# The first two sums of a seven-product weight chunk, formed ahead of the splits and into a tile of their own

## The chip, the cores and the metric

One core of one Trainium2 chip runs the whole program in one launch. The metric is the device time of an execution in microseconds (us), less being better. Five engines work side by side, each on its own queue and in the order of that queue: PE (TensorE, the matmuls; PEld is its loading of stationary operands), DVE (VectorE), ACT (ScalarE), POOL (GpSimd) and SP (SyncE, which here only issues transfers). An instruction that has to wait holds up all that stands behind it on the same engine. SBUF is the on-chip memory with 128 partitions, PSUM the banks into which matmuls accumulate.

## The reference

The kernel computes one layer on 256 tokens of width 2048, in float32: a token mixer with retention (8 heads) beside a gated linear recurrence, a merge of the two, an attention over 256 memory tokens, and a gated convolutional feed-forward part of width 5632. Nearly all of its arithmetic is products of a 256-row activation with a large weight matrix:

```python
q, k, v, g_ret, xr, yr, g_a, g_b = jnp.split(hn @ w_in[l], offsets, axis=-1)
...
merged = (jax.nn.sigmoid(g_a) * (ret_out @ w_proj_ret[l])
          + jax.nn.sigmoid(g_b) * (rnn_out @ w_proj_rnn[l]))
h = h + merged @ w_mix_out[l]
...
h = h + memory_cross_attention(hn, mem_n, xa_w_q[l], xa_w_k[l], xa_w_v[l], xa_w_o[l])
...
h = h + conv_gated_ffn(hn, ffn_w_up[l], ffn_conv_w[l], ffn_conv_b[l], ffn_w_down[l])
return rmsnorm(h, final_norm_w)
```

## The kernel before

**Products.** A weight chunk is loaded as float32 into a tile `raw`. Every value is split into two parts that a matmul can take: ACT copies it into the shorter type (`hi`, line 451), and DVE subtracts that from the value (`lo`, line 452). This is `weight_parts`. Activations are split likewise (`s`, `ts`). A product of two split operands costs three matmuls of 512 columns: high by high, low by high, high by low. The last of the three reads the weight's `lo`.

**Pairs and seven-product chunks.** Most weights are taken two column blocks of 512 at a time (`pair`, `steps_pair`). A chunk of such a pair holds two row tiles of 128 by two column blocks, four blocks in all. An ordinary chunk needs eight products, 24 matmuls. In chunks that the table `MARKS` names, the 2-by-2 product is formed with seven products, 21 matmuls, from sums of the blocks; the activation's sums (`ts`, made through a small tile `tq`) are formed by `sums_of`, the weight's by DVE. Where DVE and ACT form the weight's sums from the loaded chunk alone, `seven_parts` does it: 49 chunks. (Two other kinds get some sums by a transfer that adds; they are not touched.) In a seven-product chunk `raw` holds b11, b12, b22, b21. The seven pairs of parts are used by PE in the order p1, p3, p2, q1, q3, q2, q4. p1, p3 and p2 are splits of b11, b22 and b21; q1 and q3 split b11+b12 and b12+b22; q2 and q4 split the two sums that are built on those.

**Buffers.** `raw` has 3 buffers, `hi` and `lo` 6 each. A chunk's load is asked for on SP two chunks ahead, and it can start when DVE has formed the last `lo` from the buffer's chunk of three before. The pool `tp` gives all small temporary tiles named `tmp` (2 KB a partition each): `tq`, the two parts of attention probabilities `ps`, the junk output of squares `junk`, the gated product `ft` and `fo`, and others.

**Order.** Matmuls keep the order of the program. DVE, ACT, POOL and SP get their order from a scheduler that goes by its own estimate of durations, by priorities and by which buffers it takes to be free, so a small edit can move instructions far from it.

**Ends of pairs.** When a pair of column blocks is done, DVE gathers the banks (`o`, lines 627 and 638, called `o` in the profile). A result that the next product needs as its left operand is turned: `by_dma` has ACT split it into half words (`pl`, line 664), SP issues a transposing transfer for each 128 rows (`pt`, line 665), and ACT joins the halves again (`f`, line 677) before they are split into `s`. At the merge, lines 1083 and 1140 stand between the gathering and `pl`; at a residual, line 1155 adds the result to the stream (`nat`), and `squares` (line 1176, `junk`) takes the row sums.

Of the kernel before, what the change touches and what calls it, by code (L numbers as in the profile page):

```python
# [9 lines left out]
F32 = mybir.dt.float32  # L10
# [4 lines left out]
ALU = mybir.AluOpType  # L15
AX = mybir.AxisListType

P = 128
# [10 lines left out]
BW = 512  # L29
KC = 4  # L30
KH = 2
# [168 lines left out]
def hybrid_layer(  # L200
# [17 lines left out]
    act, dve, pe, pool, sp = nc.scalar, nc.vector, nc.tensor, nc.gpsimd, nc.sync  # L218

    cp = ctx.enter_context(tc.tile_pool(name="cp", bufs=1))  # L220
    wp = ctx.enter_context(tc.tile_pool(name="wp", bufs=2))
    bp = ctx.enter_context(tc.tile_pool(name="bp", bufs=31))
    tp = ctx.enter_context(tc.tile_pool(name="tp", bufs=7))
    sp_ = ctx.enter_context(tc.tile_pool(name="sp", bufs=2))
    pm = ctx.enter_context(tc.tile_pool(name="pm", bufs=3, space=bass.MemoryType.PSUM))
    px = ctx.enter_context(tc.tile_pool(name="px", bufs=2, space=bass.MemoryType.PSUM))
# [3 lines left out]
    def nm(s):  # L230
        count[0] += 1
        return f"{s}_{count[0]}"

    def big(shape, dt=F32, s="b"):
        return bp.tile(shape, dt, tag="big", name=nm(s))
# [120 lines left out]
    def prefetch(n):  # L356
        while len(ahead) < n and taken[0] < len(stream):
# [72 lines left out]
            if isinstance(c, tuple) and c[2] == 1:  # L430
                ahead.append(((row, c), seven_parts(raw)))
                continue
# [13 lines left out]
    def weight_parts(src, pieces_=None):  # L446

        n = src.shape[1]
        hi, lo = (wp.tile([P, KH, BW], F32R, tag=a, bufs=PART_BUFS, name=nm(a)) for a in ("hi", "lo"))
        for cs in pieces_ or (slice(0, n),):  # L450
            act.copy(hi[:, cs], src[:, cs])  # L451
            dve.tensor_tensor(out=lo[:, cs], in0=src[:, cs], in1=hi[:, cs].bitcast(F32), op=ALU.subtract)  # L452
        return [(hi[:, i, :], lo[:, i, :]) for i in range(n)]
# [12 lines left out]
    def seven_parts(raw):  # L466

        b11, b12, b22, b21 = (raw[:, i : i + 1, :] for i in range(4))
        p1, p3 = weight_parts(raw[:, 0:3:2])
        (p2,) = weight_parts(raw[:, 3:4])  # L470
        two = b12.to_broadcast([P, 2, BW])
        for o, a, b in ((raw[:, 0:2], two, raw[:, 0:3:2]), (b22, b11, b22), (b21, b22, b21)):
            dve.tensor_tensor(out=o, in0=a, in1=b, op=ALU.add)  # L473
        q1, q3 = weight_parts(raw[:, 0:2])
        q2, q4 = weight_parts(raw[:, 2:4])
        return [p1, p3, p2, q1, q3, q2, q4]

# [62 lines left out]
    def gemm_n(*args):  # L540
        return ended(steps_n(*args))
# [98 lines left out]
    def pair(*args):  # L640
        return ended(steps_pair(*args))
# [284 lines left out]
    for g in range(2):  # L926
        dec = big([P, 4, S], s="dec")
        vs, turned = [], ([], [])
        for b, o in enumerate((O_Q, O_K)):
# [6 lines left out]
            if b and not g and paired():  # L936
                a, v = pair("w_in", 0, xs, NT, O_K, O_V + BW)
                scaled(a, rs0)
                by_dma(a, rotate_both)
            else:  # L940
                a = gemm_n("w_in", 0, xs, NT, o + g * BW) if g + b else q0
                turned_rows(a, rs0, rotate_both, 2 - b if g + b else 3, g + b > 0, LAG["by_rotate"])
            if b == 1:
                sp.dma_start(
                    out=dec,
# [11 lines left out]
        for a in pair("w_in", 0, xs, NT, c, c + BW):  # L957
            t = big([P, 2, BW], s="gate")
# [466 lines left out]
    for kind, b, *n in ff_plan():  # L1425
# [5 lines left out]
        else:  # L1431
            final = b + n[0] == NF // 4
            if final:
                wfin = []
                for i in range(2):
                    t = big([P, 2, BW], s="wf")
                    sp.dma_start(
                        out=t.rearrange("p a n -> p (a n)"),
# [42 lines left out]
```

## Time and profile before

| | |
|---|---|
| median of 3 runs | 1955.75 us (1953.15 to 1957.33) |
| the profiled execution | 1956.59 us, of which its span 1954.5 us |
| PE busy | 1944.4 us, 99%, 8735 matmuls |
| DVE busy | 1659.0 us, 85% |
| ACT busy | 1457.7 us, 75% |
| POOL busy | 68.5 us, 4% |
| read from memory | 407.27 MB, 209 GB/s over the span |
| chain that ended last | PE 88%, DVE 5%, ACT 3%, DMA 2% |

The span runs from the first to the last instruction that the profiler saw; 2.1 us of the profiled execution lie around it. Busy time is the union of an engine's instructions. A matmul's end is modelled and overlaps the start of the next one, so a short pause between two matmuls may not show as idle time. In a row of the timeline the columns are the start, the length, the engine, the line, the operation, what it writes and reads, and how many like it follow each other without a break; in brackets stands the idle time ahead of it and what ended it. A group's row gives its total, the mean of one in ns, and the idle time ahead.

### The profile page before, as it was taken

The page shows a single profiled execution, that of the slowest core. Times are in us where ns is not written, and L with a number is a line of the kernel's source. Part 1 is how long each engine was busy: PE and PEld are TensorE (multiplying, and loading weights), DVE is VectorE, ACT ScalarE, POOL GpSimd, SP SyncE. Part 2 cuts the span into 40 slices and gives each one's busy share as a digit, 9 for nine tenths or more (in the row PEclk, how much of TensorE's full clock was granted, in tenths as well). Part 3 has the DMA queues.
Part 4 walks back from the last instruction along what each step waited for, and adds up shares of the span by engine and source line. Part 5 has one row for each costly group of instructions (what it writes and reads, how often), then busy time and mean ns, then how long its engine had stood idle before and what let it go on. Part 6 is the DMA issues. An engine that isn't in the chain of part 4 may idle for free.

```text
span 1954.5 us, 24287 instructions
## 1 busy us (share of the span) xinstructions
PE 1944.4 (99%) x8735; PEld 1612.9 (83%) x8735; DVE 1659.0 (85%) x2155; ACT 1457.7 (75%) x1792; POOL 68.5 (4%) x69
## 2 busy tenths in 40 slices
PE   9999999999999999999999999999999999999998
PEld 7888888888888888888888888888887888888887
DVE  6887987787889988887888857789999889999986
ACT  6665758999756666778678777888877578884784
POOL 0000001000100000000000000000000000000000
PEclk9999999999999999999999999999999999999999
DMA  8866767666867786778868687676677877678773
GB/s 332 262 215 198 245 222 217 213 218 229 237 217 265 233 264 215 253 253 252 247 213 239 223 221 225 226 232 226 211 224 224 269 248 221 223 224 271 230 255 119
DMA packets 211352, 454.99 MB, mean 233 GB/s; under 512 B 143264, under 2 KB 147872, under 8 KB 170400
## 3 DMA queue, kind: packets, MB, share of 16 engines
q1 hardware_dynamic: 204896, 430.38, 66.5%
q0 software_dynamic: 6336, 23.07, 6.3%
q8 instruction: 68, 1.11, 0.2%
q14 instruction: 52, 0.43, 0.1%
HBM read 407.27 MB, written 2.10 MB: 209 GB/s over the span
## 4 chain that ended last, share of the span: by engine, by line
PE 88%; DVE 5%; ACT 3%; DMA 2%; issue 2%; POOL 0%; SPq 0%; POOLq 0%; DVEq 0%; ACTq 0%
PE acc L285 63%; PE sm L285 26%; DVE lo L452 2%; ACT hi L451 1%; DMA raw<-in_wall 1%; ACT f L677 1%; DVE o L627 1%; ACT pl L664 0%; DMA fl<-fr 0%; DVE o L638 0%; DMA pt<-pl 0%; DVE raw L473 0%; DVE fv L1282 0%; DVE fg L1282 0%; DVE s L702 0%
## 5 line engine op out<-in xcount | busy, mean ns | idle before, releaser
L452 DVE TENSOR_TENSOR lo<-raw,hi 128x1024 fp32r<-128x1024 f32 (+1 forms) x824 | 940.4, 1169 | 203.0 <-ACT hi L451 193.0
L285 PE MATMUL acc<-hi,s 128*128 128x512 f32 x3526 | 1081.5, 388 | 0.4 <-ACT s L727 0.2
L451 ACT CAST hi<-raw 128x1024 fp32r<-128x1024 f32 (+1 forms) x824 | 801.1, 1007 | 301.9 <-DMA raw<-in_wall 83.1
L285 PEld LDWEIGHTS acc<-hi,s 128*128 128x128 f32 x3526 | 659.5, 188 | 136.1 <-DVE s L728 0.6
L285 PE MATMUL acc<-lo,s 128*128 128x512 f32 x1727 | 669.7, 388 | 0.1
L285 PE MATMUL sm<-hi,s 128*128 128x512 f32 x1464 | 450.9, 389 | 0.0
L285 PEld LDWEIGHTS acc<-lo,s 128*128 128x128 f32 x1727 | 324.4, 188 | 68.6 <-DVE lo L452 2.1
L285 PEld LDWEIGHTS sm<-hi,s 128*128 128x128 f32 x1464 | 274.7, 188 | 57.2 <-ACT prob L1203 0.2
L285 PE MATMUL sm<-lo,s 128*128 128x512 f32 x720 | 280.3, 389 | 0.0
L677 ACT COPY f<-pt 128x1024 uint16<-128x1024 uint16 x128 | 166.8, 1353 | 10.0 <-DMA pt<-pl 10.0
L285 PEld LDWEIGHTS sm<-lo,s 128*128 128x128 f32 x720 | 135.2, 188 | 28.6 <-DVE lo L452 0.6
L285 PE MATMUL acc<-hi,ts 128*128 128x512 f32 x438 | 134.9, 389 | 0.0
L473 DVE TENSOR_TENSOR raw<-raw 128x1024 f32<-128x1024 f32 x147 | 127.1, 865 | 1.9
L285 PEld LDWEIGHTS acc<-hi,ts 128*128 128x128 f32 x438 | 82.2, 188 | 17.0
L285 PE MATMUL acc<-lo,ts 128*128 128x512 f32 x219 | 85.7, 391 | 0.7 <-DVE lo L452 0.6
L664 ACT COPY pl<-o 128x1024 uint16<-128x1024 uint16 x64 | 62.5, 1040 | 3.7 <-DVE o L638 2.8
L330 POOL DMA_DIRECT2D tw<-in_wall x24 | 21.4, 891 | 980.8 <-DMA tw<-in_wall 355.7
L285 PEld LDWEIGHTS acc<-lo,ts 128*128 128x128 f32 x219 | 41.1, 188 | 10.8 <-DVE lo L452 2.4
L664 ACT COPY pl<-rows 128x1024 uint16<-128x1024 uint16 x44 | 43.7, 1044 | 7.6 <-DVE rows L694 7.6
L1421 ACT ACTIVATE o<-o,ro 128x512 f32<-128x512 f32 x44 | 30.1, 718 | 23.9 <-DVE o L638 23.8
L638 DVE TENSOR_TENSOR o<-o,sm 128x512 f32<-128x512 f32 x64 | 42.2, 679 | 3.9 <-PE sm L285 3.9
L285 PE MATMUL sm<-hi,ts 128*128 128x512 f32 x146 | 45.0, 389 | 0.0
(197 smaller groups left out, 1321.2 us busy)
## 6 DMA issues: line engine op xcount, KB each, us to landing
raw<-in_wall SPq DMA_DIRECT2D x319, 1024.0 KB, 5.1
raw<-in_wall SPq DMA_DIRECT2D x24, 768.0 KB, 5.6
tw<-in_wall SPq DMA_DIRECT2D x24, 512.0 KB, 7.7
tw<-in_wall POOLq DMA_DIRECT2D x24, 512.0 KB, 7.3
raw<-in_wall SPq DMA_DIRECT2D x13, 512.0 KB, 6.6
fr<-in_wall SPq DMA_DIRECT2D x12, 512.0 KB, 7.4
fl<-fr POOLq DMA_DIRECT2D x12, 512.0 KB, 8.1
nat<-in_x SPq DMA_DIRECT2D x8, 512.0 KB, 9.7
```

The source lines that it names most:

```text
L285: tc.keep_in_program_order(pe.matmul(*a, **k))
L330: pool.dma_start(out=far[i], in_=source(i)[:, 0:KH, :], accum_op=ALU.add)
L451: act.copy(hi[:, cs], src[:, cs])
L452: dve.tensor_tensor(out=lo[:, cs], in0=src[:, cs], in1=hi[:, cs].bitcast(F32), op=ALU.subtract)
L473: dve.tensor_tensor(out=o, in0=a, in1=b, op=ALU.add)
L627: dve.tensor_tensor(out=o, in0=a, in1=b, op=op)
L638: dve.tensor_tensor(out=o, in0=o, in1=a, op=ALU.add)
L664: act.copy(planes[:, tt], words[:, tt])
L677: act.copy(halves_[:, :, :, cs], turned_[:, :, :, cs])
L1421: act.mul(a[:, tt, :], a[:, tt, :], rs2[:, tt : tt + 1])
```

## The change

`seven_parts` now begins with the two first sums, b11+b12 and b12+b22, in one DVE instruction of the same shape as before, and writes them into a new tile `t13` (128 by 1024 float32, 4 KB a partition, one buffer). Before, they were formed after the splits of p1, p3 and p2 and overwrote b11 and b12. The two later sums are as before, but the first of them reads b11+b12 from `t13`. q1 and q3 are split from `t13`. The pool of small temporary tiles goes from 7 to 5, which frees as much memory as the new tile takes. No instruction is added or removed.

```diff
-    tp = ctx.enter_context(tc.tile_pool(name="tp", bufs=7))
+    tp = ctx.enter_context(tc.tile_pool(name="tp", bufs=5))
...
         b11, b12, b22, b21 = (raw[:, i : i + 1, :] for i in range(4))
+        t = wp.tile([P, KH, BW], F32, tag="t13", bufs=1, name=nm("t13"))
+        dve.tensor_tensor(out=t, in0=b12.to_broadcast([P, KH, BW]), in1=raw[:, 0:3:2], op=ALU.add)
         p1, p3 = weight_parts(raw[:, 0:3:2])
         (p2,) = weight_parts(raw[:, 3:4])
-        two = b12.to_broadcast([P, 2, BW])
-        for o, a, b in ((raw[:, 0:2], two, raw[:, 0:3:2]), (b22, b11, b22), (b21, b22, b21)):
-            dve.tensor_tensor(out=o, in0=a, in1=b, op=ALU.add)
-        q1, q3 = weight_parts(raw[:, 0:2])
+        for o, x, y in ((b22, t[:, 0:1], b22), (b21, b22, b21)):
+            dve.tensor_tensor(out=o, in0=x, in1=y, op=ALU.add)
+        q1, q3 = weight_parts(t)
         q2, q4 = weight_parts(raw[:, 2:4])
```

The order of the matmuls stays. DVE, ACT, SP and, in one place, POOL get another order, and not only inside `seven_parts`. Lines behind the edit count one higher afterwards. Three places follow.

The first is the merge, ahead of the first product with `w_mix_out` (at 805 us in the trace of before). DVE before (o_6749 is the result that is turned first, raw_6852 an ordinary chunk, raw_6886 a seven-product one):

```order
L638 TENSOR_TENSOR o_6749<-o_6749,acc_6498 128x1024
L1140 TENSOR_TENSOR o_6750<-o_6750,o_5363 128x1024
L1083 SCALAR_TENSOR_TENSOR o_6749<-o_6109,o_6749 128x1024
L452 TENSOR_TENSOR lo_6855<-raw_6852,hi_6854 128x1024
L1140 TENSOR_TENSOR o_6749<-o_6749,o_5362 128x1024
L452 TENSOR_TENSOR lo_6859<-raw_6852,hi_6858 128x1024
L452 TENSOR_TENSOR lo_6889<-raw_6886,hi_6888 128x1024
```

And now on DVE (o_6762 is that result, raw_6865 and raw_6899 the two chunks):

```order
L639 TENSOR_TENSOR o_6762<-o_6762,acc_6510 128x1024
L1141 TENSOR_TENSOR o_6763<-o_6763,o_5372 128x1024
L1084 SCALAR_TENSOR_TENSOR o_6762<-o_6120,o_6762 128x1024
L452 TENSOR_TENSOR lo_6872<-raw_6865,hi_6871 128x1024
L1141 TENSOR_TENSOR o_6762<-o_6762,o_5371 128x1024
L470 TENSOR_TENSOR t_1325_6901<-raw_6899 128x1024
L452 TENSOR_TENSOR lo_6904<-raw_6899,hi_6903 128x1024
```

The ordinary chunk's second `lo` has moved ahead of the merge's last addition, and the first sum stands ahead of its chunk's first `lo`. On SP, a chunk's load that stood between the two transposes of this result now stands ahead of both.

The second place is the first residual (at 850 us). DVE before (o_7018 and nat_6931 belong to the column block that is turned first, raw_7242 and raw_7321 are seven-product chunks):

```order
L638 TENSOR_TENSOR o_7018<-o_7018,acc_6849 128x1024
L559 TENSOR_TENSOR tq_7182<-g_7179,tq_7182 128x128
L1155 TENSOR_TENSOR nat_6931<-nat_6931,o_7018 128x1024
L562 TENSOR_TENSOR ts_7181<-tq_7182,ts_7181 128x512
L452 TENSOR_TENSOR lo_7215<-raw_7208,hi_7214 128x1024
L452 TENSOR_TENSOR lo_7245<-raw_7242,hi_7244 128x1024
L473 TENSOR_TENSOR raw_7242<-raw_7242 128x1024
L473 TENSOR_TENSOR raw_7242<-raw_7242 128x512
L452 TENSOR_TENSOR lo_7249<-raw_7242,hi_7248 128x512
L473 TENSOR_TENSOR raw_7242<-raw_7242 128x512
L452 TENSOR_TENSOR lo_7256<-raw_7242,hi_7255 128x1024
```

And now on DVE (nat_6945, raw_7256 and raw_7336 are the same three):

```order
L639 TENSOR_TENSOR o_7032<-o_7032,acc_6862 128x1024
L452 TENSOR_TENSOR lo_7229<-raw_7222,hi_7228 128x1024
L1156 TENSOR_TENSOR nat_6945<-nat_6945,o_7032 128x1024
L470 TENSOR_TENSOR t_1397_7258<-raw_7256 128x1024
L452 TENSOR_TENSOR lo_7261<-raw_7256,hi_7260 128x1024
L474 TENSOR_TENSOR raw_7256<-t_1397_7258,raw_7256 128x512
L452 TENSOR_TENSOR lo_7265<-raw_7256,hi_7264 128x512
L474 TENSOR_TENSOR raw_7256<-raw_7256 128x512
L452 TENSOR_TENSOR lo_7271<-t_1397_7258,hi_7270 128x1024
L729 SCALAR_TENSOR_TENSOR s_7383<-xt_7041,pb,s_7383 128x256
L470 TENSOR_TENSOR t_1412_7338<-raw_7336 128x1024
L452 TENSOR_TENSOR lo_7275<-raw_7256,hi_7274 128x1024
```

The residual's addition now stands behind one more `lo` (and behind the split of `ts`, above these rows), and the next seven-product chunk's first sum stands ahead of this chunk's last `lo`. Of the 49 first sums, 24 stand ahead of at least one `lo` of an earlier chunk in this way.

ACT at the same place, before:

```order
L451 CAST hi_7244<-raw_7242 128x1024
L664 COPY pl_7192<-nat_6931 128x1024 x2
L664 COPY pl_7199<-nat_7025 128x1024 x2
L451 CAST hi_7248<-raw_7242 128x512
L451 CAST hi_7255<-raw_7242 128x1024
L1176 ACTIVATE junk_7470,ss_6848<-nat_6931 128x512
L1176 ACTIVATE junk_7472,ss_6848<-nat_6931 128x512
L1176 ACTIVATE junk_7508,ss_6848<-nat_7025 128x512
L451 CAST hi_7259<-raw_7242 128x1024
```

And now on ACT:

```order
L451 CAST hi_7260<-raw_7256 128x1024
L665 COPY pl_7206<-nat_6945 128x1024 x2
L451 CAST hi_7264<-raw_7256 128x512
L665 COPY pl_7213<-nat_7039 128x1024 x2
L451 CAST hi_7270<-t_1397_7258 128x1024
L1177 ACTIVATE junk_7486,ss_6861<-nat_6945 128x512
L728 ACTIVATE s_7383<-xt_7041,pb 128x256
L451 CAST hi_7274<-raw_7256 128x1024
```

Two of the squares have moved back, behind the rows shown, and one cast has moved in between the two pairs of `pl`.

The third place is an end of a pair in the feed-forward part (at 1624 us). DVE before (raw_13732 is the first chunk of the next pair, o_13713 and o_13712 the results of the pair that ends):

```order
L452 TENSOR_TENSOR lo_13735<-raw_13732,hi_13734 128x1024
L562 TENSOR_TENSOR ts_13674<-tq_13675,ts_13674 128x512
L627 TENSOR_TENSOR o_13713<-o_13712,acc_13539 128x512
L1282 SCALAR_TENSOR_TENSOR fv_13117<-f_13658,pf,fv_13117 128x254
L627 TENSOR_TENSOR o_13712<-o_13713,acc_13540 128x512
L1291 TENSOR_TENSOR fo_13726<-ft_13725,fv_13117 128x512
L627 TENSOR_TENSOR o_13713<-acc_13540,o_13712 128x512
L627 TENSOR_TENSOR o_13713<-acc_13540,o_13713 128x512
L638 TENSOR_TENSOR o_13713<-o_13713,sm_13449 128x512
L638 TENSOR_TENSOR o_13713<-o_13713,sm_13448 128x512
L702 TENSOR_TENSOR s_13729<-fo_13726,s_13729 128x2x256
L452 TENSOR_TENSOR lo_13739<-raw_13732,hi_13738 128x1024
```

And now on DVE (lo_13773 is the former lo_13735):

```order
L563 TENSOR_TENSOR ts_13712<-tq_13713,ts_13712 128x512
L628 TENSOR_TENSOR o_13751<-o_13750,acc_13576 128x512
L1283 SCALAR_TENSOR_TENSOR fv_13152<-f_13696,pf,fv_13152 128x254
L628 TENSOR_TENSOR o_13750<-o_13751,acc_13577 128x512
L1292 TENSOR_TENSOR fo_13764<-ft_13763,fv_13152 128x512
L628 TENSOR_TENSOR o_13751<-acc_13577,o_13750 128x512
L628 TENSOR_TENSOR o_13751<-acc_13577,o_13751 128x512
L703 TENSOR_TENSOR s_13767<-fo_13764,s_13767 128x2x256
L639 TENSOR_TENSOR o_13751<-o_13751,sm_13484 128x512
L639 TENSOR_TENSOR o_13751<-o_13751,sm_13485 128x512
L452 TENSOR_TENSOR lo_13773<-raw_13770,hi_13772 128x1024
```

The next pair's first `lo` has moved from ahead of the gathering to behind it.

## The prediction

> **What bounds the kernel now.** I read the page's busy times first, then the windows of start, body and end, then the chain, and then the matmuls' starts in the timeline.
>
> ```profile
> PE 1944.4 (99%) x8735; PEld 1612.9 (83%) x8735; DVE 1659.0 (85%) x2155; ACT 1457.7 (75%) x1792; POOL 68.5 (4%) x69
> ...
> 0.00:15.00 15.00, 13.71 (x53) 10.72 (x54) 8.54 (x19) 9.00 (x18) 0.97 (x7) 1.00 0.85 298
> 15.00:1940.00 1925.00, 1923.39 (x8625) 1595.11 (x8624) 1644.65 (x2117) 1446.40 (x1772) 65.30 (x58) 1.00 0.73 233
> 1940.00:1955.00 15.00, 7.32 (x62) 7.11 (x60) 5.82 (x22) 2.25 (x4) 2.21 (x4) 0.90 0.36 140
> ...
> 96.18 2.72 PE sm L285 x12
> ...
> 212.49 0.49 PE L285 MATMUL acc<-lo,s 128*128 128x512 f32 x1
> 212.82 0.62 PE L285 MATMUL acc<-hi,s 128*128 128x512 f32 x2
> ...
> 1531.88 0.61 PE L285 MATMUL acc<-hi,ts 128*128 128x512 f32 x2
> 1532.87 0.50 PE L285 MATMUL acc<-lo,ts 128*128 128x512 f32 x1 [0.38 <-DVE lo L452]
> ```
>
> The second number of a window is its length, the third PE's busy time. Of the 10.1 us in which PE is idle, 1.3 lie in the first 15 us and 7.7 in the last 15 (the output); the body has 1.6. The chain's row gives the pace: 12 matmuls in 2.72 us, 0.227 each. A matmul is drawn 0.39 long, so a pause can hide 0.16. I therefore counted starts: between 15 and 1940 us, 21 pauses bring consecutive starts 0.3 us or more apart, the first at 212.49, the last the one behind 1532.87. Their excess over 0.227 adds up to 4.1 us. That is all that better supply of PE can win: 0.21% of the time. The change neither removes matmuls nor moves them, and 0.2%, 3.9 us, is about what a measurement of this kernel can tell from no change.
>
> The Trainium skill's page "Perfetto Trace Analysis", section "Identifying the Most-Contended Engine", says that the matmul busy share is no good measure of how close PE is to its roofline, since pipelined matmuls look smaller in the trace. By that rule the 99% would leave more to win; the pace of the starts, which needs no ends, says that it doesn't here.
>
> **What the change costs inside a chunk: nothing.** The durations:
>
> ```profile
> L452 DVE TENSOR_TENSOR lo<-raw,hi 128x1024 fp32r<-128x1024 f32 x745 | 889.4, 1220 | 199.5 <-ACT hi L451 189.7 <-PE acc L285 4.2 <-PE sm L285 2.1
> L473 DVE TENSOR_TENSOR raw<-raw 128x512 f32<-128x512 f32 x98 | 67.3, 687 | 1.4
> L473 DVE TENSOR_TENSOR raw<-raw 128x1024 f32<-128x1024 f32 x49 | 59.8, 1219 | 0.5
> ...
> DVE lo L452 <- ACT hi L451: 195.4, 139, 6.7
> ACT hi L451 <- DVE raw L473: 45.0, 40, 4.5
> ```
>
> 49 first sums of 1.22 us, 98 others of 0.69: the same instructions before and after, on operands of the same size. What is gained is overlap. The first sum no longer waits for ACT's cast, so DVE can use the 1.05 us that ACT needs, where it now stands (195 us of such waits), and ACT waits less for sums (45 us). What is lost is that p1's and p3's `lo` come one sum, 1.2 us, later, with PE using them first. DVE works on a chunk for 4 wide instructions (the first sum and the `lo`s of p1 with p3, q1 with q3, q2 with q4) x 1.22 and 3 narrow ones (`lo` of p2, two sums) x 0.69, 6.9 us; its 21 matmuls take 21 x 0.227 = 4.8. So where DVE works just ahead of PE, it is the late parts, q1 to q4, that PE is likely to wait for, and those come no later. Only where PE stands does either matter.
>
> **A gain of 0.5 us at 1532.** Here two seven-product chunks follow each other, starting with a late landing:
>
> ```profile
> 1518.96 1.05 ACT L451 CAST hi<-raw 128x1024 fp32r<-128x1024 f32 x1 [5.67 <-DMA raw<-in_wall]
> 1529.86 1.06 ACT L451 CAST hi<-raw 128x1024 fp32r<-128x1024 f32 x1 [2.30 <-PE acc L285]
> ...
> 1520.04 1.23 DVE L452 TENSOR_TENSOR lo<-raw,hi 128x1024 fp32r<-128x1024 f32 x1 [3.28 <-ACT hi L451]
> 1531.60 4.77 DVE L452 TENSOR_TENSOR lo<-raw,hi 128x1024 fp32r<-128x1024 f32 x4
> ```
>
> DVE runs without a break from 1520.04 to the `lo` at 1531.60 that ends the pause at 1532.87. With the first sum at 1518.96 it is 1.08 us ahead. But the cast that goes before that `lo` gets its buffer from PE at 1529.86, so the `lo` ends no earlier than 1529.86 + 1.06 + 1.22 = 1532.14 against 1532.82: 0.68 earlier, of which the pause (0.76 less 0.23) takes 0.5.
>
> **A loss of 0.5 us at the merge.** One `lo` moved ahead of the last addition there.
>
> ```profile
> 804.67 1.22 DVE L1140 TENSOR_TENSOR o<-o,o 128x1024 f32<-128x1024 f32 x1
> ...
> 805.92 3.89 ACT L664 COPY pl<-o 128x1024 uint16<-128x1024 uint16 x4 [0.80 <-DVE o L1140]
> 816.50 1.35 ACT L677 COPY f<-pt 128x1024 uint16<-128x1024 uint16 x1 [1.48 <-DMA pt<-pl]
> ...
> 806.99 1.23 SPq L665 DMA_TRANSPOSE pt<-pl  x1
> 808.32 0.53 SPq L256 DMA_DIRECT2D raw<-in_wall  x1
> ...
> 820.16 1.01 PE L285 MATMUL acc<-hi,s 128*128 128x512 f32 x2
> ```
>
> This is the only place where the whole chain DVE, `pl`, transposes, `f`, split ends at a waiting PE (820.16, two matmuls in 1.01 where 0.62 is usual). The addition comes one `lo` pitch, 1.13 us, later. The load that SP issues between the two transposes (0.53 and its gaps, 0.6) moves ahead of both, where its buffer is free before `pl` is. So the second transpose starts 1.13 - 0.6 = 0.5 late, and PE with it. Bounds: -0.6, if the load's traffic is out of the way sooner, and 1.2.
>
> **A loss of 0.6 us behind the residual.** `nat` now stands behind a `lo` and a split of `ts`:
>
> ```profile
> 847.71 1.21 DVE L1155 TENSOR_TENSOR nat<-nat,o 128x1024 f32<-128x1024 f32 x1
> 848.85 0.68 DVE L562 TENSOR_TENSOR ts<-tq,ts 128x512 fp32r<-128x512 f32 x1
> 849.45 2.35 DVE L452 TENSOR_TENSOR lo<-raw,hi 128x1024 fp32r<-128x1024 f32 x2
> ...
> 849.31 3.88 ACT L664 COPY pl<-nat 128x1024 uint16<-128x1024 uint16 x4
> 854.57 0.62 ACT L1176 ACTIVATE junk<-nat 128x512 f32<-128x512 f32 x1
> 860.32 1.36 ACT L677 COPY f<-pt 128x1024 uint16<-128x1024 uint16 x1
> 870.36 1.99 ACT L451 CAST hi<-raw 128x1024 fp32r<-128x1024 f32 x2
> ...
> 871.42 2.36 DVE L452 TENSOR_TENSOR lo<-raw,hi 128x1024 fp32r<-128x1024 f32 x2
> ...
> 872.71 0.50 PE L285 MATMUL acc<-lo,ts 128*128 128x512 f32 x1
> ```
>
> `nat` ends 0.60 + 1.13 = 1.73 later, at 850.65, and `pl` starts 1.34 later than 849.31. From there ACT works almost without a break to the cast at 870.36, whose `lo` (end 872.65) PE takes at 872.71. Two of four squares (0.62 each) now stand behind that cast: 1.34 - 1.24 = 0.1 later. But the transposes start 1.34 later too. If the second half needs 7.6 us from issue to `f`, as at the merge (808.90 to 816.50), `f` starts at 860.6 rather than about 859.9, another 0.7 (0.2 if it is quicker). Together 0.3 to 0.9; 0.6. Bounds -0.3 (the pause of 0.1 goes) and 2.
>
> **A loss of 0.4 us at 1630.** The next pair's first `lo` moved behind the gathering:
>
> ```profile
> 1623.59 1.22 DVE L452 TENSOR_TENSOR lo<-raw,hi 128x1024 fp32r<-128x1024 f32 x1
> 1630.51 1.22 DVE L452 TENSOR_TENSOR lo<-raw,hi 128x1024 fp32r<-128x1024 f32 x1
> ...
> 1630.26 0.39 PE L285 MATMUL acc<-lo,s 128*128 128x512 f32 x1
> ```
>
> The first row is that `lo`, the second the next one. Without the first, DVE gets through the same work 1.13 sooner than 1630.51: the moved `lo` runs from 1629.38 to 1630.60 and PE, which takes it at 1630.26, waits 0.4. The second then ends at 1631.7, as before.
>
> **Elsewhere** I take 0.3: other `lo`s that moved back by 0.5 to 1.6 us reach PE with as much or more to spare, a few with 0.1 to 0.4. Cover: had PE not the parts ready some microseconds ahead, each moved sum would cost its 1.2.
>
> **Sum:** -0.5 + 0.5 + 0.6 + 0.4 + 0.3 = +1.3 us against the profiled execution's 1956.59 (span 1954.5 and 2.1 around it): 1957.9. That execution lies 0.8 above the median of the runs, 1955.75; in their terms 1957.0.
>
> **Rivals.**
>
> *The sums block DVE.* 24 of the 49 first sums stand ahead of `lo`s of earlier chunks and wait at DVE's head for their own chunk's landing; before, they stood behind two `lo`s.
>
> ```profile
> ACT hi L451 <- DMA raw<-in_wall: 83.1, 63, 5.7
> ```
>
> ACT waits for landings 63 times, 1.3 us each; if DVE stands that long at 24 places, PE feels those where it has less than 1.3 us to spare. At four places that makes 4 x 1.3 = 5.2 and, with the sum, 1957.0 + 5.2 = 1962.2. It decides from landings some 2 us later than the order assumes. Against it: spare time of several microseconds at most places. Chance 0.36, with all else that ends above +0.2%.
>
> *The overlap wins.* The pauses from 1488 to 1533 (2.0 us of the 4.1) go and the three losses hide: 1955.75 - 2.0 = 1953.7. For it: the waits of DVE on ACT. Against it: all other pauses have other causes. Chance 0.2, of which 0.06 beyond -0.2%, which needs every pause gone or a lucky median.
>
> *The smaller pool binds.* The skill's page named above, section "Optimization Strategy", says that a gap that repeats may mean too few buffers; by it the two tiles are better kept, and their loss would show as new gaps. The trace has one place with six in use:
>
> ```profile
> L285 PE MATMUL acc<-v,ps x48: 389/389/389, 1129.9 to 1173.2; 128*128 128x512 f32 x48
> L1241 DVE TENSOR_TENSOR ps<-f,ps x3: 680/681/689, 1110.9 to 1169.6; 128x512 fp32r<-128x512 f32 x3
> ```
>
> The third pair's `lo` would wait for the first pair's matmuls, from 1129.9 on, while its own are due at 1146; it has moved back on DVE by four `lo`s. If it held DVE the 2 us of those matmuls with nothing to spare behind: 1959.0; chance 0.03, counted below with what lies within 0.2%.
>
> **Numbers.** Likeliest: 1957.0, with a chance of 0.41 by itself. Within 0.2% lie, beside it, the smaller win of the overlap (0.14) and the smaller pool (0.03): together 0.58; faster by more 0.06, slower by more 0.36. The range runs from 1953.5, the overlap's win, to 1963.0, a little over the blocked sums.
>
> **What would show it.** Right: PE's starts 0.5 later at the merge, `lo` behind the gathering at 1630, a shorter pause near 1532, and fewer waits of ACT on the sums. Wrong: new idle time of DVE ahead of line 470 with pauses of PE right behind it, or a body with under 1 us of pauses.

## The result, and the profile after

The changed kernel takes 1961.55 us, median of 6 runs (1958.06 to 1963.76), against 1955.53 of the kernel before beside it: ratio 1.0031, 95% interval [1.0019, 1.0042]. It is slower by 6.0 us. The range of the prediction holds that; its likeliest case, 1957.0, doesn't, and the rival that was to end on the other side, 1962.2, does.

The profiled execution took 1961.12 us with a span of 1959.3, 4.8 more than before's span. The page's busy times and chain, and the waits of PE and of DVE (columns: us in total, times, longest):

```profile
PE 1944.7 (99%) x8735; PEld 1614.2 (82%) x8735; DVE 1656.8 (85%) x2155; ACT 1456.5 (74%) x1792; POOL 68.3 (3%) x69
PE 72%; DVE 11%; ACT 8%; issue 5%; DMA 3%; SPq 0%; POOL 0%; DVEq 0%; POOLq 0%; ACTq 0%
...
PE acc L285 <- DVE lo L452: 4.1, 3, 2.7
PE acc L285 <- DMA fl<-fr: 1.1, 1, 1.1
...
PE acc L285 <- DVE s L703: 0.6, 1, 0.6
...
DVE t L470 <- DMA raw<-in_wall: 22.4, 14, 5.2
```

No engine has more work. What is new is the last row: DVE stands 14 times, 22.4 us in all, at a first sum whose chunk has not landed, and PE's waits for a `lo` have gone from 0.6 to 4.1 us. As the matmuls stand in the same order in both kernels, the start of the n-th in one trace can be set against the n-th in the other. The lag of after behind before grows so, from place to place (times of after; a row ends at the start that ends the place's last larger step, so a tenth or two can fall to the row below):

| place | lag gained, us |
|---|---|
| start, to 12 us | -0.97 |
| 146 to 252 | +0.96 |
| 270 | +0.26 |
| 512 (the transfer `fl`) | +0.53 |
| 820 to 901 (merge, residual) | -0.78 |
| 1459 to 1503 | -1.69 |
| 1532 | -0.66 |
| 1628 | +0.87 |
| 1769, the pause | +3.01 |
| 1773 to 1777, matmuls at half pace | +1.55 |
| 1915 to 1920 | +1.62 |
| the rest | +0.14 |

The first row lies ahead of the first of the 49 sums, which runs at 94 us. One place, the pause at 1769 with the slow matmuls behind it, adds 4.56, against a net lag of 4.84; the other rows lose 4.4 and win 4.1. In the timeline of DVE there, then of PE, then in the chain:

```profile
1764.49 0.42 DVE L558 TENSOR_TENSOR tq<-g 128x256 f32<-128x256 f32 x1
1770.13 1.23 DVE L470 TENSOR_TENSOR t<-raw 128x1024 f32<-128x1024 f32 x1 [5.22 <-DMA raw<-in_wall]
1771.28 2.35 DVE L452 TENSOR_TENSOR lo<-raw,hi 128x1024 fp32r<-128x1024 f32 x2
...
1769.21 0.61 PE L285 MATMUL acc<-hi,ts 128*128 128x512 f32 x2
1772.55 0.50 PE L285 MATMUL acc<-lo,ts 128*128 128x512 f32 x1 [2.72 <-DVE lo L452]
...
1759.84 10.27 DMA raw<-in_wall
...
1771.28 1.23 DVE lo L452
1772.51 0.04 issue
1772.55 2.53 PE acc L285 x7
```

This is the 44th of the 49 seven-product chunks. Its first sum came to the head of DVE's queue at 1764.9 and waited 5.22 us for the landing. Three `lo`s of earlier chunks, whose own inputs were there, stood behind it, and PE needed the first of them at 1769.7. It got it at 1772.55: 3.11 us from start to start instead of 0.227. The load had taken 10.3 us, where the page gives 5.0 as the median of such loads; two transfers that add to memory (`nat`, from POOL) ran beside it, but that they slowed it was not tried. Behind the pause the granted clock fell, as the windows show (the column ahead of the last two is the clock):

```profile
1700.00:1769.00 69.00, 69.00 (x307) 57.11 (x306) 62.51 (x83) 50.27 (x61) 2.61 (x3) 1.00 0.79 240
1773.30:1776.80 3.50, 3.50 (x10) 2.72 (x10) 3.46 (x6) 2.61 (x4) 0.00 (x0) 0.54 0.98 314
```

Eight matmuls follow each other there at 0.43 us.

### The profile page after: what moved, and what is told of

It reads as the page before. It is cut to its first block, busy times and chain, and to the rows that moved or that the text cites. A ratio compares the mean times of both kernels' runs of the same rounds, so it can differ in the third digit from the quotient of the medians.

```text
span 1959.3 us, 24295 instructions
## 1 busy us (share of the span) xinstructions
PE 1944.7 (99%) x8735; PEld 1614.2 (82%) x8735; DVE 1656.8 (85%) x2155; ACT 1456.5 (74%) x1792; POOL 68.3 (3%) x69
## 4 chain that ended last, share of the span: by engine, by line
PE 72%; DVE 11%; ACT 8%; issue 5%; DMA 3%; SPq 0%; POOL 0%; DVEq 0%; POOLq 0%; ACTq 0%
PE acc L285 50%; PE sm L285 22%; DVE lo L452 4%; ACT hi L451 3%; DMA raw<-in_wall 3%; ACT f L678 1%; DVE fv L1283 1%; DVE o L628 1%; DVE o L639 1%; ACT pl L665 1%; DVE s L703 1%; DVE raw L474 0%; DVE xr L1051 0%; DMA fl<-fr 0%; DVE fg L1283 0%
## 5 line engine op out<-in xcount | busy, mean ns | idle before, releaser
L452 DVE TENSOR_TENSOR lo<-raw,hi 128x1024 fp32r<-128x1024 f32 (+1 forms) x775 | 882.6, 1168 | 172.3 <-ACT hi L451 169.1
L451 ACT CAST hi<-raw 128x1024 fp32r<-128x1024 f32 (+1 forms) x775 | 750.4, 1005 | 265.9 <-PE acc L285 64.5
L470 DVE TENSOR_TENSOR t<-raw 128x1024 f32<-128x1024 f32 x49 | 59.9, 1223 | 22.5 <-DMA raw<-in_wall 22.4
L452 DVE TENSOR_TENSOR lo<-t,hi 128x1024 fp32r<-128x1024 f32 x49 | 59.9, 1222 | 19.6 <-ACT hi L451 19.6
L451 ACT CAST hi<-t 128x1024 fp32r<-128x1024 f32 x49 | 51.4, 1050 | 17.3 <-PE acc L285 7.5
```

The source lines that it names most:

```text
L470: dve.tensor_tensor(out=t, in0=b12.to_broadcast([P, KH, BW]), in1=raw[:, 0:3:2], op=ALU.add)
```

## The experiments

Two theories were set against each other. **A:** the loss is a blocked head: a first sum that waits for its landing holds up `lo`s that are ready, above all at 1770. **B:** the loss is the sum of the many small moves in the order of DVE and ACT. Later rivals stand with the runs. Each batch had its own runs of the kernel before; a ratio is of a kernel's runs to those.

### The 44th sum held back

`issue_after` queues an instruction behind another one on its engine, without a wait for it to finish. `last_lo` is the last `lo` formed so far in the program; `nth` counts the chunks.

```diff
-        dve.tensor_tensor(out=t, ...)
+        nth[0] += 1
+        with tc.issue_after(last_lo[0]) if nth[0] == 44 else nullcontext():
+            dve.tensor_tensor(out=t, ...)
```

> The changed kernel with one difference: the first sum of the 44th of the 49 chunks (the one for which DVE waited 5.22 us at 1770) is queued behind the last lo of the chunk before it. Theory A (one blocked head makes the loss): the pause of 3.11 us between matmuls at 1769 goes, and with it the slow stretch behind it (8 matmuls 0.43 apart instead of 0.227, 1.6 us); 2.9 + 0.1 + 1.6 = 4.6 us less than the changed kernel's 1961.55, so about 1957.0, ratio to before 1.0008. Rival B (the loss is spread over the many instructions that were moved, or PE would wait there for the landing anyway): at least 1960.0, ratio 1.0023 or more, with another pause within a few us of 1769.

1957.34 us, ratio 1.0009 [1.0000, 1.0017]. The order differs from the changed kernel's only around this place, and 4.2 of the 6.0 us are gone. Its DVE at the place:

```profile
1764.66 2.35 DVE L452 TENSOR_TENSOR lo<-raw,hi 128x1024 fp32r<-128x1024 f32 x2
...
1770.00 1.22 DVE L475 TENSOR_TENSOR t<-raw 128x1024 f32<-128x1024 f32 x1
```

Two `lo`s run at once, the sum comes when its chunk is there, 0.13 us earlier than in the changed kernel, and PE has no pause there. What is left: pauses of 1.04, 0.74 and 1.09 us between 1912 and 1916, 0.81 at 252 and 1.34 at 513.

### The 44th chunk alone

The converse: the kernel before, `seven_parts` as it was, with the new form for one chunk (and its tile, and the pool at 5).

```diff
-                ahead.append(((row, c), seven_parts(raw)))
+                nth[0] += 1
+                form = seven_first if nth[0] == 44 else seven_parts
+                ahead.append(((row, c), form(raw)))
```

> The kernel before with one difference: the 44th chunk alone takes the new form (its first sum first, into t13; the small pool at 5), and stands there ahead of three lo's of earlier chunks, as in the changed kernel. Theory A: this one instruction at the head of DVE's queue makes PE pause about 3 us near 1770 and slows it behind: 1955.5 + 4.6 = 1960.1, ratio 1.0023. Rival B (many small moves): within 1 us of before, 1955.0 to 1956.5.

1960.97 us, ratio 1.0026 [1.0017, 1.0035]: one instruction, put ahead of three, makes most of the loss of the whole change.

```profile
1769.57 1.23 DVE L482 TENSOR_TENSOR t<-raw 128x1024 f32<-128x1024 f32 x1 [3.76 <-DMA raw<-in_wall]
...
1771.98 0.79 PE L285 MATMUL acc<-lo,ts 128*128 128x512 f32 x1 [2.54 <-DVE lo L452]
...
1771.90:1775.10 3.20, 3.12 (x8) 2.50 (x9) 3.20 (x6) 0.47 (x1) 0.00 (x0) 0.52 0.62 207
```

DVE waits 3.76 us, PE 2.54, and the clock falls to 0.52. Theory A holds for this place, B doesn't.

### The 44th sum behind two of the three

```diff
+        with tc.issue_after(last_lo[-3]):       # behind the first two of the older lo's
             dve.tensor_tensor(out=t, ...)
```

> The kernel before with the new form in the 44th chunk alone, as in the run that had that alone, but its first sum stands behind the first two of the three older lo's instead of ahead of them. DVE still waits at its head for the landing, but with one older lo behind it instead of three. Theory A: what counts is what stands behind the waiting sum and when PE is due to take it. The first two lo's are there in time; the third is due later than the landing at about 1769.6 plus two instructions, or by less than 1 us: 1955.5 to 1957, ratio 1.0000 to 1.0008, a pause under 1 us. Rival (the wait itself costs, wherever the sum stands): 1960, ratio 1.0023.

1956.12 us, ratio 1.0001 [0.9992, 1.0010]. DVE still waits at its head, but nothing that is due stands behind it:

```profile
1771.29 1.23 DVE L492 TENSOR_TENSOR t<-raw 128x1024 f32<-128x1024 f32 x1 [1.98 <-DMA raw<-in_wall]
```

PE's starts stay within 0.34 us of each other from there to 1779.5. A pause of 0.92 us follows at 1779.88, at a `lo` of DVE; whether it comes from the wait isn't shown (with the 34th and 35th chunk alone in the new form there is one of 0.46 near it). As far as the times tell, the wait costs nothing by itself; what it holds up does.

### The same hold without a landing

The kernel before, with useless work in DVE's queue instead of a wait (the results go into a tile like `t13`, with the pool at 5):

```diff
+        for _ in range(4):
+            with tc.issue_after(last.ins):
+                last = dve.tensor_tensor(out=idle, in0=raw[:, 1:3], in1=raw[:, 1:3], op=ALU.add)
```

> The kernel before with four useless sums (128x1024, 1.22 us each) put into DVE's queue at 1767 us, ahead of the three lo's that stood behind the waiting first sum; their results are not used. DVE is then held there by 4.5 us of work instead of by a wait for a landing. Theory A (only the hold of DVE counts): the lo that PE takes at 1771.0 in the trace of before ends at about 1773.2; PE pauses some 2.3 us from start to start, and as pauses of 2.38 us and more were followed by 8 or 9 matmuls at 0.43 instead of 0.227, and pauses up to 1.61 us were not, 1.6 us more by the slow stretch: 1955.5 + 2.1 + 1.6 = 1959.2, ratio 1.0019; without a slow stretch 1957.6, ratio 1.0011. Rival (DVE catches up, or PE isn't waiting for DVE there): within 0.5 us of before.

1959.83 us, ratio 1.0021 [1.0012, 1.0030]. PE pauses 3.81 us at 1770.2, more than the 2.3 expected, since DVE came to the place 0.9 us later than in the trace of before and PE 0.6 earlier; then eight matmuls at 0.43 or close to it.

```profile
1774.04 0.50 PE L285 MATMUL acc<-lo,ts 128*128 128x512 f32 x1 [3.42 <-DVE lo L463]
```

The hold without a landing costs 4.5 us, the 44th chunk alone 4.9: holding DVE there is enough, no landing is needed.

### The changed kernel again

> The changed kernel itself, unaltered, on the chip of this batch. Theory A (the wait at 1770 is set by the order and comes in every execution): 1960.5 to 1962.5, ratio 1.0025 to 1.0035, again a wait of DVE of 4.5 to 6 us ahead of the first sum at 1770, a pause of PE of 2.5 to 3.5 us there and 7 to 9 matmuls at 0.43 behind it. Rival (that execution had a late landing by chance): a pause under 1.5 us there and a time nearer to 1957.

1961.81 us, median of 6 (1958.24 to 1964.18), ratio 1.0038 [1.0026, 1.0050]. The profiled execution was the quickest of the six, 1958.24. The blocked head comes again, but shorter:

```profile
1768.17 1.23 DVE L470 TENSOR_TENSOR t<-raw 128x1024 f32<-128x1024 f32 x1 [4.21 <-DMA raw<-in_wall]
...
1770.59 0.50 PE L285 MATMUL acc<-lo,ts 128*128 128x512 f32 x1 [1.28 <-DVE lo L452]
...
1770.00:1777.00 7.00, 6.41 (x28) 5.33 (x29) 6.97 (x10) 3.05 (x4) 0.00 (x0) 1.00 0.78 272
```

The pause is 1.67 us from start to start and the clock stays at 1.00. So the pause comes in both executions, its size doesn't: the expectation of 2.5 to 3.5 us missed. The two executions differ by 2.88 us; the pause (1.44) and the slow stretch (1.55) make up 2.99; the other pauses differ too, and nearly cancel.

### All sums held back

```diff
+        with tc.issue_after(last_lo[0]):
             dve.tensor_tensor(out=t, ...)
```

> The changed kernel with every first sum queued behind the last lo of the chunk before it, so that none can hold a lo of an earlier chunk. Theory A: no pause of PE over 1.5 us is left, DVE's waits ahead of the first sums stay but nothing that PE needs stands behind them; 1956 to 1957.5, ratio 1.0003 to 1.0010. Rival C (the overlap wins once nothing is blocked): the pauses between 1459 and 1533 go as in the changed kernel, 2.1 us, and no new ones come: 1953.5, ratio 0.9990. Rival B: 1960 or more.

1957.55 us, ratio 1.0007 [0.9998, 1.0016]. The time is near the expected, the reason given for it fell: one pause over 1.5 us is left, of 2.38 at 1911, and with it a slow stretch. It isn't a blocked sum; PE waits for the low part of the first of the last two gated products:

```profile
1913.75 0.71 PE L285 MATMUL acc<-hi,s 128*128 128x512 f32 x1 [2.00 <-DVE s L708]
...
1910.74 2.35 DVE L452 TENSOR_TENSOR lo<-raw,hi 128x1024 fp32r<-128x1024 f32 x2
1913.01 0.68 DVE L708 TENSOR_TENSOR s<-fo,s 128x512 fp32r<-128x512 f32 x1
...
1911.29 1.22 DVE L452 TENSOR_TENSOR lo<-raw,hi 128x1024 fp32r<-128x1024 f32 x1
1912.42 0.68 DVE L702 TENSOR_TENSOR s<-fo,s 128x512 fp32r<-128x512 f32 x1
```

The first row is PE's, the next two are DVE's in this kernel, the last two DVE's in the kernel before. DVE's order around the last gated product has changed: here two `lo`s follow each other ahead of the split, before, a row of the convolution stood between them. In the changed kernel the order there is a third one, with a `lo` between the second product and its split, and that is where it loses its 1.62 at 1915 to 1920. Theory A doesn't explain this second place; B does. Which of the moved rows costs what was not separated.

### The last chunks in the old form

To undo that second place alone, the last two chunks keep the old form, with the 44th sum held:

```diff
+        return seven_parts(raw) if nth[0] < 48 else seven_old(raw)
```

> The changed kernel with the 44th chunk's first sum held behind the older lo's, and in addition the last two of the 49 chunks in the old form, which gives DVE the order of before for the last 93 instructions. Theory A (what is left of the loss with the 44th held lies in the moved rows at the last gated product): the pauses between 1912 and 1917, which come to 2.4 us with the 44th chunk held alone, go; 1957.3 - 2.4 = 1954.9, ratio 0.9995. Rival B (the rest of the loss lies in the many other moves): 1957 or more, ratio 1.0006 or more, with pauses elsewhere.

1955.84 us, ratio 0.9998 [0.9989, 1.0007]: the pauses behind 1629 are gone, and 1.5 us with them (2.4 expected). With the 44th sum held and two chunks as before, the 47 others in the new form cost nothing that can be told from zero. In the medians the two places make up the loss: 4.2 and 1.5 of 6.0. The 4.2 is clear of the noise; the 1.5 is not (the intervals of the two ratios overlap), and rests on the pauses that went.

The same with every sum held, and the last four chunks in the old form:

> The kernel with every first sum held behind the last lo of the chunk before it, but with the last four of the 49 chunks in the old form, so that the last gated product has the order of before on DVE and ACT. Theory A (its 1957.55 came from one place, the pause of 2.38 us at 1911 with eight slow matmuls behind it, 2.2 + 0.2 + 1.6 = 4.0 us in its trace): 1957.55 - 4.0 = 1953.6, ratio 0.9990, faster than both kernels. Rival B (the pauses come back at other places): 1955 to 1957, ratio 0.9998 to 1.0008.

1952.70 us (1951.19 to 1955.71), ratio 0.9990 [0.9982, 0.9999]: faster than both kernels, by 2.7 us against before in the medians, though the interval only just leaves out 1. The profiled execution was the slowest of its eleven, 1955.71, with a wait for `fl` that comes in every kernel at a size of its own:

```profile
513.50 0.50 PE L285 MATMUL acc<-fl,s 128*128 128x512 f32 x1 [1.54 <-DMA fl<-fr]
```

There are no pauses in it behind 991 us but one of 0.34 at 1532. Which of the pauses of before it does without in its usual executions is therefore left open.

Set beside the others, this trace shows one thing more: the changed kernel has, most likely, a second blocked sum that PE feels, at 232 us.

```profile
232.52 1.23 DVE L470 TENSOR_TENSOR t<-raw 128x1024 f32<-128x1024 f32 x1 [2.61 <-DMA raw<-in_wall]
...
250.78 1.22 DVE L452 TENSOR_TENSOR lo<-t,hi 128x1024 fp32r<-128x1024 f32 x1
...
252.05 0.50 PE L285 MATMUL acc<-lo,ts 128*128 128x512 f32 x1 [0.59 <-DVE lo L452]
```

From that sum to the `lo` at 250.78 no wait of DVE is listed (19.07 us busy of 19.50), so the delay is handed on, and PE pauses 0.98 us for that `lo`. The four traces in which this sum waits, 2.60 to 2.82 us, all have this pause, 0.81 to 1.23 us; no other trace has it. In the kernel with every sum held and four chunks in the old form, DVE waits for no landing there, runs the same `lo` 2.44 us sooner, and PE doesn't pause. With every sum held and no chunk in the old form, DVE stands 3.54 us for a cast at 231 instead, and a pause of 1.28 us comes at 233. So the wait most likely makes the pause; no run held that one sum alone.

### The pool alone, and two chunks alone

```diff
-    tp = ctx.enter_context(tc.tile_pool(name="tp", bufs=7))
+    tp = ctx.enter_context(tc.tile_pool(name="tp", bufs=5))
```

> The kernel before with the pool of small temporary tiles at 5 instead of 7 and nothing else; 10 rows on DVE move, none on the other engines. Theory A: no difference, 1955.0 to 1956.2, ratio 0.9997 to 1.0004. The prediction's rival (the smaller pool binds at the attention, 1121 to 1146 us): 2 us more, 1957.5, ratio 1.0010, with a new pause of PE there.

1955.03 us, ratio 0.9997 [0.9988, 1.0005]; no pause between 900 and 1490 us. The pool by itself isn't a cause.

> The kernel before with the new form in the two chunks that follow each other at 1517 to 1533 (the 34th and 35th) and nowhere else. Theory A (the overlap is real where DVE and ACT work just ahead of PE): the pause near 1530 to 1532, 0.65 us over the usual pitch in the trace of before, 0.4 and 1.05 in two others with the old form there, goes; 1955.5 less 0.5 to 0.9: about 1954.8, ratio 0.9996, which the times alone can hardly tell, the pauses can. Rival: the 34th sum waits for its landing at the head of DVE's queue (3.08 us in the changed kernel) and the pause stays or grows.

1955.58 us, ratio 0.9997 [0.9988, 1.0006]. No pause of 0.3 us or more is left between 1504 and 1750, so the one at 1532 went; the times don't tell it, as expected.

### The tile without the early sum

The sum goes into `t13`, but is queued behind the split of p2, and in a second kernel behind the split of p1 and p3 only:

```diff
         p1, p3 = weight_parts(raw[:, 0:3:2])
+        first = last_lo[0]
         (p2,) = weight_parts(raw[:, 3:4])
+        with tc.issue_after(first):             # the other kernel: last_lo[0], p2's
+            dve.tensor_tensor(out=t, ...)
```

> The changed kernel's tile t13 and small pool, but each first sum back behind the split of p2, where it stood before, by its place in the program and on DVE's queue. Theory A (the harm is the sum's place at the head of the queue, not the tile): no wait of DVE ahead of a first sum, no pause of PE at 1770, 1955 to 1957, ratio 0.9998 to 1.0007. Rival T (the tile itself, with its one buffer held from the sum to the split of q1 and q3, costs by waits of a sum for the split of the chunk before): 1958 or more, with DVE idle ahead of the sums.

1960.38 us, ratio 1.0023 [1.0014, 1.0031]. The expectation of A fell. But in the kernel before, 19 of the 49 sums stand on DVE ahead of p2's split, here none, so this run mixed two things; hence the second (with 20 ahead of it):

> The changed kernel's tile t13 and small pool, but each first sum is queued behind the split of its own chunk's p1 and p3 only, which is all that overwriting them demanded before (the earlier run of this kind put it behind p2's split too, later than before). This is the tile by itself. Theory A (the harm of the change is the place of the sum at the head of the queue, not the tile): as before, 1955 to 1956.5, ratio 0.9997 to 1.0005, no pause of PE over 1.1 us but that at 512. Rival T (the tile with one buffer costs by itself): 1958 or more, with DVE idle ahead of first sums. Rival P (the order that the scheduler makes around any new tile costs by small moves): 1957 to 1960 with several pauses of 0.5 to 1.5 us at places of their own.

1958.73 us, ratio 1.0021 [1.0011, 1.0031]. A fell again: there is no wait at a sum, yet it is slow. In its profiled execution, 1960.91 and so 2.2 us over the median, pauses of 0.71 to 1.27 us are new against the trace of before, or were a tenth of that, at 1419, 1505, 1759 and 1919, and those at 820, 872 and 1534 are longer: rival P. The tile, with the sum held to where it had to be before, gives the scheduler an order that costs 3.4 us. Why, and what its single buffer has to do with it, stays open; DVE is nowhere idle ahead of a first sum, so not by waits for the buffer.

## Why the prediction was right in its range and wrong in its likeliest case

**What bounds the kernel: right.** The matmuls, their order and their pace of 0.227 stayed, and the loss lies in pauses between starts (and, not foreseen, in a stretch of slow ones). One reading is off without effect: the last window of 15 us reaches 0.5 us past the span, so 7.2 us of idle time lie there, not 7.7. That better supply can win 4.1 us was read from one execution: the kernel with the small pool alone, all but ten of whose rows on DVE stand as before, has 2.6 us of such pauses in its trace. Of the 1.69 won from 1459 to 1503, some 1.5 is then scatter: that kernel has 0.35 us of pauses there, before 1.9.

**Inside a chunk, nothing: right,** as far as the last runs tell: with two places mended the new form costs nothing.

**1532, -0.5: right.** With the old form there, five traces show 0.41 to 1.05 us of pauses; with the new one and the sum early, seven show 0 to 0.23.

**The merge, +0.5: wrong sign.** The addition came later, by 1.56 us on the clock and 0.8 against PE, and yet `f` was early:

```profile
806.23 1.23 DVE L1141 TENSOR_TENSOR o<-o,o 128x1024 f32<-128x1024 f32 x1
...
808.56 4.51 SPq L666 DMA_TRANSPOSE pt<-pl  x3
...
815.93 1.36 ACT L678 COPY f<-pt 128x1024 uint16<-128x1024 uint16 x1
```

From the addition to the second `f` it takes 9.7 us, before 11.8 (804.67 to 816.50). The step that failed is the one that let the load between the two transposes count only by its time on SP's queue. With the load ahead, the transposes follow each other and are done sooner: the six traces with that order on SP take 9.7 to 9.8 us from the addition to the second `f`, the six with the load between the transposes 10.4 to 11.8. That was the lower bound, -0.6. The pause of 0.4 is in none of the first six, but two of the other six don't have it either, so part of the gain is scatter.

**The residual, +0.6: wrong.** The pauses at 873 and 901, 0.1 to 0.2 us, went. The working moved `nat` back by what now stands ahead of it, but began its sum at 846 us. DVE came to this place sooner than before:

```profile
836.43 2.36 DVE L452 TENSOR_TENSOR lo<-raw,hi 128x1024 fp32r<-128x1024 f32 x2 [1.95 <-ACT hi L451]
...
834.80 2.36 DVE L452 TENSOR_TENSOR lo<-raw,hi 128x1024 fp32r<-128x1024 f32 x2
```

The first row is before's, with 1.95 us of waiting ahead of it; the second is after's, without. `nat` ran at 847.98 against 847.71, not 1.73 later. A sum over moved rows must begin at the last wait ahead of them, not in a run of busy ones.

**1630, +0.4: right in place and sign.** 1.1 us of pause in the changed kernel's first trace, 0.7 in its second, 0 to 0.5 in four variants with the new form there; but the run with useless work, which has before's order there, shows 0.75 too, so part of it is scatter.

**Elsewhere, +0.3: mis-sized.** The pause at 252 gave 0.9, those at 1915 to 1920 1.6. The first most likely belongs to the rival of blocked sums, the second lies at a gated product that the prediction never looked at.

**The rival of blocked sums: right in kind, wrong in make-up.** It priced four places at the mean landing wait of 1.3 us, 5.2 us. There were 14 waits, most of them free; one place with a wait of 4 to 5 us made 4.2 us of the median, part of it by a slow clock that the trace of before had not shown, and the wait of 2.6 us at 232 most likely made the 0.9 at 252. That the total fits, 1962.2 against 1961.55, is luck in part. The step that failed is its weight, 0.36 against "spare time of several microseconds at most places": a mean and a "most" where each place had to be looked at, so that 1957.0 and not 1962.2 became the likeliest case. The trace of before held the answer. The 44th chunk landed there at 1771.8 (the cast that waits for it):

```profile
1771.79 1.57 ACT L451 CAST hi<-raw 128x1024 fp32r<-128x1024 f32 x2 [1.17 <-DMA raw<-in_wall]
...
1771.02 0.39 PE L285 MATMUL acc<-lo,ts 128*128 128x512 f32 x1
```

A sum of 1.2 us from there, and a `lo` of 1.2 behind it, end at 1774.1; PE took that `lo` at 1771.02. The difference, 3.1 us, is close to the 2.88 us by which the pause of 3.11 exceeded the usual pitch.

**The smaller pool, 0.03: rightly small.**

## What to carry to other kernels

Before an instruction that waits for a transfer is let forward on an in-order queue, set the landing that the trace shows for that very transfer against the moment at which the consumer takes what will now stand behind it, place by place; a mean of waits or of spare time says nothing about the one place that decides. When a scheduler has the last word, a dependence taken away is a freedom given to it: give it with a fence of order only (behind the last older `lo`, no wait added), which here turned 6.0 us of loss into 1.3 (the 44th sum held, ratio 1.0009) or 1.5 (all held, 1.0007). Not every fence does that: behind a split of the sum's own chunk it left 3.4 and 4.9 us. And when a local edit moves rows far away, look for the second loss there: here it lay 70 us behind the last chunk that was edited (1845 to 1915).

## What the runs showed of the hardware

A pause of PE cost more than its length once it passed about 2 us. In these traces pauses of 1.67 and 1.93 us from start to start left the clock at full rate; those of 2.38, 2.93, 3.11 and 3.81 were each met by a stretch of 3.41 us at a granted clock of 0.50, with 7 or 8 matmuls at or near 0.43 us, which adds 1.4 to 1.6 us. The stretch doesn't begin with the pause's end: behind the one of 3.81 it starts 1.2 us after the matmuls do (1775.25 against 1774.04), with the 44th chunk alone 0.4 us ahead of them (1771.55 against 1771.98). The window of the kernel with all sums held, behind its pause of 2.38:

```profile
1913.70:1917.20 3.50, 3.45 (x8) 2.73 (x9) 2.56 (x4) 2.52 (x3) 0.00 (x0) 0.52 0.89 293
```

The Trainium skill's page "TensorE: Matmul & The Clock Gate", section "Part 1: The HAM clock gate (the "warmup" mystery)", says that the array falls to half its clock after an idle window of about 3.4 us and returns to full after about 3.4 us of work. The way back agrees with the 3.41 us of the slow stretches here. The way down doesn't: 2.00 us without a matmul in flight by the modelled ends (the wait in the row at 1913.75) was enough.
